# A decoder step's last stage: another order of its hand-written queues, other rooms for its weights, and per-layer inputs loaded ahead

## The chip, the cores and the metric

The kernel runs on one core of a Trainium2 chip, in one launch. The metric is device time in microseconds of that core. The version before was run three times: median 2211.37 us, 2208.99 to 2212.40. One more execution was recorded by the hardware profiler. It took 2207.24 us; all times "at" some microsecond below count from the start of its span of 2205.2 us.

The engines are TensorE (PE in the profile, its weight loads PEld), VectorE (DVE), ScalarE (ACT), GpSimd (POOL) and SyncE (SP), which here only issues DMAs. Each works through its own list in order.

## The reference, cut to what matters

The reference is one layer of a decoder: attention in two groups, a gated MLP with a short convolution, and a gate by per-layer inputs, for 1024 prompt tokens and 64 sample tokens. The change lies in the last two steps, the MLP's product with `w_down` and the per-layer gate:

```python
y = (jax.nn.silu(conv) * c) @ lw['ffn_w_down']
...
h = h + y
h = h + (p @ lw['ple_w_proj']) * jax.nn.sigmoid(rmsnorm(h, lw['g_ple']) @ lw['ple_w_gate'])
```

`h` is 1024 tokens by 1024 columns, `p` 1024 by 256, `ple_w_gate` 1024 by 1024, `ple_w_proj` 256 by 1024, all float32.

## The kernel before, in words

**Products.** A float32 product is done as three products of rounded parts: an operand is split into a high part (a cast, mostly on ScalarE) and a low part (operand minus high part, on VectorE), and `mm3` (L160 to L163) multiplies high by high, high by low and low by high. Both `w_down` and `ple_w_gate` are multiplied by a scheme of seven products of quarter matrices in place of eight, with sums and differences of quarters as operands.

**The down pass** (loop over `steps`, from L2388) does its seven products one after the other, in the order `SEVEN`, each in eleven steps `k`. Step `k` multiplies for four tiles of 128 tokens, `t` = 0 to 3. The last product is `p == 4`. Its steps 9 and 10 are done together, tile by tile. After each tile's last step `folded` adds the sum from PSUM to `h` (L2330), on VectorE. Between the steps of this last product the kernel already prepares the next stage: `square` and `root` make the row scales of the norm (ScalarE, then GpSimd), `turn_first` transposes a first quarter of `h` (`xg`, `r11`), and `ple_in(c)` brings in one of two chunks of the per-layer inputs: three DMAs into tiles named `pin` (two of four token tiles, one of the 64 sample rows), transposes on TensorE (L2364), splits into `ph`, `pl` and `pts`. Chunk 0 is called at `k == 5`, chunk 1 after tile 0 of the last step. Each `ple_in` issues its own loads, into the three rooms of the `stage` ring. After the loop four `square`, `root` and four stores `dh<-h` (L2436) follow.

**The last stage** multiplies by `ple_w_gate`. Its instructions are put in by name: `later(name, make)` notes a step, and the string `LAST` (L39) lists all names. Inside `manual_schedule` the steps of TensorE, ScalarE, VectorE and GpSimd keep the order of that string on their engine. SyncE isn't in that list; the order of its DMAs is the compiler's choice, as is where the instructions outside `LAST` (`ple_in`, `turn_first`) come in between. The names that matter:

| name | engine | what it does |
|---|---|---|
| `P1t` to `P7t` | TensorE | product 1 to 7 for tile t: 12 matmuls of 512 columns |
| `Yt`, `Tbt`, `Tat` | TensorE | turns of three quarters of `h`, four transposes each, all into the three banks `pd` |
| `Jnt`, `sA`, `sB`, `sJf` | TensorE | projection of `p` (6 matmuls); sample rows (8, 8 and 4 matmuls) |
| `ryt`, `rat`, `Ut` | ScalarE | copies from banks to `h`: of `Yt` (L2542), of `Tat`, of `P1t` |
| `it`, `et`, `gt`, `jt` | VectorE | sums and differences of turned quarters; `it`, `et` read the bank of `Tbt` |
| letter + `c` or `l` + number | ScalarE / VectorE | high and low part of an operand (`ac0`/`al0` of tile 0, `wc0`/`wl0` of a weight row block) |
| `JL`, `W`, `C`, `Z`, `V`, `N`, `X` | SyncE | loads of weights (`wp`, `wn`), 512 KB each |
| `csk`, `ck`, `zk`, `vk`, `nk` | ScalarE / VectorE | scale by the gain and subtract quarters of weights |
| `jc0_`, `jl0_` | ScalarE / VectorE | parts of `ple_w_proj`, 1024 columns |
| `Cq`, `Cs`, `Cm`, `Ca`, `Co` | VectorE, ScalarE, SyncE | sum, sigmoid, times projection, plus `h`, store |
| `sk0`, `sd0` | VectorE / ScalarE | empty the bank of `sJ0` |

**Rooms.** The weight loads go through four rooms in turn (`pair`, L2444): `gb` in the pool `hp`, `pc` in the pool `pl`, and two rooms of the down pass, `place_of(10)` and `r4`. The n-th load takes room n modulo 4, and waits until whoever used that room before is done with it. The pool `pl` is opened when the down pass's pool `wf` is closed, over the same memory: `sg`, `wj`, the rooms `q3k` and `q2k` of the split weights, and `pc` last. Banks of PSUM come from four small rings: `pd` (three banks), `pm` (two), `p2t` (two), `p2` (one). `turn_first` and `ple_in` take theirs from `p2t`.

Of the kernel before, what the change touches and what calls it, by code (L numbers as in the profile page):

```python
# [8 lines left out]
F32 = mybir.dt.float32  # L9
# [9 lines left out]
P = 128  # L19
D = 1024  # L20
T = 1024
NT = 8
NB = 8
TS = 8
R = NB * TS
# [13 lines left out]
LAST = (  # L39
# [13 lines left out]
VIAP = 20  # L53
GS0 = 1
NWB = 10
# [11 lines left out]
def step_kernel(ctx: ExitStack, tc: tile.TileContext, A):  # L67
    nc = tc.nc
    pe, act, dve, pool, sp = nc.tensor, nc.scalar, nc.vector, nc.gpsimd, nc.sync
# [151 lines left out]
    z = {}  # L221
# [1189 lines left out]
    def stage(shape, dt, name):  # L1411
        return z["sg"].tile(shape, dt, tag="stage", name=name, bufs=3)
# [67 lines left out]
    def square(t, f):  # L1480

        rows = P if t < NT else R
        junk = z["junk"].tile([P, 512], BF16, tag="junk", name="junk")
        act.activation(junk[:rows], hrows(t)[:, f * 512:f * 512 + 512], AF.Square, scale=1.0 / 32.0,
                       accum_out=z["ss"][:rows, 2 * t + f:2 * t + f + 1])
# [7 lines left out]
    def root(t):  # L1493

        rows = P if t < NT else R
        s0, s1 = (z["ss"][:rows, 2 * t + f:2 * t + f + 1] for f in range(2))
        pool.tensor_scalar(s0, s0, s1, EPS, ALU.add, ALU.add)
        return pool.tensor_tensor(z["rs"][:rows, t:t + 1], s0, mhalf[:rows, 0:1], ALU.pow).ins
# [156 lines left out]
    def p2t(shape, name):  # L1655
        return psT.tile(shape, F32, tag="t", name=name)
# [319 lines left out]
    def later(name, make):  # L1976

        steps[name] = make
# [210 lines left out]
    def part(i, j, t):  # L2189
        return h[:, 4 * i + t, j * 512:j * 512 + 512]  # L2190

    def kept(i, j, t):
        return dh2[(4 * i + t) * P:(4 * i + t + 1) * P, j * 512:j * 512 + 512]
# [4 lines left out]
    def turn_part(i, j, t, bank, here=False):  # L2198
        pt = bank([P, 4, P], "pt")
        for k in range(4):  # L2200
            m = pe.transpose(pt[:, k], part(i, j, t)[:, k * P:(k + 1) * P], ident)
            if here and k == 0:
                tc.keep_in_program_order(m)
        return pt
# [13 lines left out]

    def turn_first(t):

        pt = turn_part(0, 0, t, p2t, True)
        xg["11", t] = x = xroom(room_tag(0, t))
        split(x[:, 0], x[:, 1], pt)
        if t % 2 == 0:
            r11[t // 2] = z["xs"].tile([P, 2, 512], F32, tag=place_of(4 + t // 2), name="r11", bufs=1)
        act.copy(v4(r11[t // 2][:, t % 2]), pt)
# [36 lines left out]
    def place_of(k):  # L2263
        return f"st{(k + 3) % NK}"
# [50 lines left out]
    def folded(p, t):  # L2315

        ps = acc[p][t]
        h11, h12, h21, h22 = (h[:, i, j:j + 512] for i in (t, t + 4) for j in (0, 512))
        if p == 1:
            act.copy(h11, ps)  # L2320
        elif p == 5:
            act.copy(h22, ps)
            act.copy(h12, ps)
        elif p == 6:
            dve.tensor_tensor(h21, h11, ps, ALU.add)
        elif p == 7:
            dve.tensor_tensor(h21, h21, ps, ALU.subtract)
        else:
            hx = {3: h12, 2: h11, 4: h21}[p]
            dve.tensor_tensor(hx, hx, ps, ALU.add)  # L2330
# [9 lines left out]
    def ple_gain():  # L2340
# [5 lines left out]
        z["gk"] = z["fb"].tile([P, 8], F32, name="gkT", tag="gkT")  # L2346
        act.copy(z["gk"], pt[:, 0:8])

    def ple_in(c):

        th, tl = (z["fq"].tile([P, T], F32R, tag="p" + s, name="p" + s, bufs=2) for s in "hl")
        cs = slice(c * P, (c + 1) * P)
        for t0 in (0, 4, 8):
            pin = stage([P, 4, P], F32, "pin")
            if t0 < NT:
                n, rows = 4, P
                sp.dma_start(pin, A["p_prompt"][0, 0, t0 * P:(t0 + 4) * P, cs].rearrange("(i p) c -> p i c", p=P))
            else:
                n, rows = 1, R
                sp.dma_start(pin[:R, 0], A["p_sample"][0].rearrange("b t c -> (b t) c")[:, cs])  # L2360
            pt = p2t([P, 512], "pt_pl")
            w = (n - 1) * P + rows
            for i in range(n):
                pe.transpose(pt[:, i * P:i * P + rows], pin[:rows, i], ident[:rows, :rows])  # L2364
            if t0 < NT:
                split(th[:, t0 * P:t0 * P + w], tl[:, t0 * P:t0 * P + w], pt[:, :w])
            else:
                ts = z["fq"].tile([P, P], F32R, tag="pts", name="pts", bufs=2)
                split(ts[:, :R], ts[:, R:], pt[:, :R])
        return th, tl, ts  # L2370
# [17 lines left out]
    for i, (p, k) in enumerate(steps):  # L2388
        if i + 4 < len(steps):
            load(*steps[i + 4])  # L2390
        if i + 2 < len(steps):
            operands(*steps[i + 2])
        if k == 0:
            acc[p] = banks(i // NK)
        q = SEVEN[i // NK - 1] if i >= NK else 0
        if p == 4 and k == NK - 2:
            continue
        for t in range(4):
            for k_ in ((k - 1, k) if p == 4 and k == NK - 1 else (k,)):
                summed(p, k_, t)  # L2400
            if k == NK - 1:
                folded(p, t)
            if p == 4 and k == NK - 1 and t == 0:
                pT.append(ple_in(1))
        if q and k in (1, 3, 5, 7):
            folded_on(q, k // 2)
        for p0, k0, i_, j_ in ((6, 2, 1, 1), (3, 3, 0, 0), (2, 1, 0, 1), (2, 2, 1, 0)):
            if p == p0 and k >= k0 and (k - k0) % 2 == 0 and k - k0 < 8:
                residue(i_, j_, (k - k0) // 2)
        if p == 1 and k == 1:  # L2410
            with tc.issue_after(opd[-1][0]):
                for half in range(2):
                    fold_sample(acc_s[half], half)
        elif p == 1 and k == 4:
            row_scale(NT)
            ple_gain()
        elif p == 1 and k == 7:
            turned_sample()
        elif p == 2 and k == 8:
            first_gate()  # L2420
        elif p == 4:
            if k in (1, 3, 5, 7):
                row_scale(k // 2)
                square(k // 2 + 4, 1)
            if k in (2, 4, 6, 7):
                turn_first((k - 1) // 2)
            if k in (6, 8):
                for t in range(4):
                    i_ = (8 - k) // 2
                    sp.dma_start(kept(i_, 1, t), part(i_, 1, t))  # L2430
            if k == 5:
                pT.append(ple_in(0))
    for t in range(4):
        square(t + 4, 0)
        root(t + 4)
        sp.dma_start(kept(1, 0, t), part(1, 0, t))  # L2436

    rw.close()
    opened("pl")
# [3 lines left out]

    def pair():  # L2444

        pool_, tag = ((z["hp"], "gb"), (z["pl"], "pc"), (z["xs"], place_of(10)), (z["xs"], "r4"))[pairs[0] % 4]
        pairs[0] += 1
        return pool_.tile([P, 2, 512], F32, tag=tag, name="wp", bufs=1)

# [56 lines left out]
        later(f"{name}l{k}", lo)  # L2506

    def tile_part(t):

        def s2():  # L2510
            return r11[t // 2][:, t % 2]
# [323 lines left out]
```

## Time and profile before

| | before |
|---|---|
| median of three runs | 2211.37 us |
| runs | 2208.99 to 2212.40 us |
| profiled execution | 2207.24 us |
| its span | 2205.2 us |
| TensorE busy, share of span | 2117.2 us, 96% |
| VectorE | 1701.4 us, 77% |
| ScalarE | 1384.4 us, 63% |
| granted TensorE clock, mean | 0.987 |

In a timeline a row gives the start, the duration, the engine and line, the operation, what it writes and reads, and how often in a row; in brackets the idle time of the engine before it and what ended that. Matmuls are pipelined: a row lasts longer than the distance to the next start, and the distance is what counts. A table by stage gives, for each stretch, the busy time and the number of instructions (in parentheses) of each engine, the granted TensorE clock (1.00 is full), the share of the DMA engines in use and their rate. A row of waits gives who waited for whom, the sum in us, how many times, and the longest. In the row of 40 slices a digit is the busy share of a slice of 55 us in tenths.

### The profile page before, as it was taken

To read this page: it belongs to the slowest core of one execution; us is meant where nothing else is said; L and a number is where in the kernel's file an instruction comes from. 1 tells how busy PE (TensorE), PEld (TensorE's weight loads), DVE (VectorE), ACT (ScalarE), POOL (GpSimd) and SP (SyncE) were. 2 spreads that over 40 slices of the span, in tenths; PEclk is the share of its full clock that TensorE was granted. 3 is DMA by queue.
4 is the path that set the end of the run, shared out by engine and by line. 5 is a ranking of instruction groups with operands and counts; after the bars stand their busy time and mean duration, and the time that the engine had idled before them with its cause. 6 is when DMAs were issued, how large, how long until landed. Compare 5 with 4: busy or idle time off the path is not lost. (4 is left out here: it accounts for less than half of the span.)

```text
span 2205.2 us, 37408 instructions
## 1 busy us (share of the span) xinstructions
PE 2117.2 (96%) x12928; PEld 1897.3 (86%) x12928; DVE 1701.4 (77%) x2611; ACT 1384.4 (63%) x3735; POOL 1207.0 (55%) x1311
## 2 busy tenths in 40 slices
PE   7999999999999999999999999999999999999799
PEld 6888978878888888887898878999999998888677
DVE  4775676467788888887788878888888886996686
ACT  5676766777778888887777776433333333534651
POOL 5675668576777777778455556565656651001100
PEclk9999999999999999999999999999999999999899
DMA  5343235412342222211421223323222226878432
GB/s 186 107 144 108 77 120 157 142 54 68 106 121 58 63 75 62 61 56 47 161 88 58 84 82 98 110 86 102 91 92 95 92 82 235 248 219 251 141 126 84
DMA packets 205952, 244.56 MB, mean 111 GB/s; under 512 B 42934, under 2 KB 137635, under 8 KB 205763
## 3 DMA queue, kind: packets, MB, share of 16 engines
q1 hardware_dynamic: 189507, 189.98, 27.3%
q0 software_dynamic: 15024, 47.72, 7.5%
q10 hardware_dynamic: 1232, 4.46, 0.5%
q8 instruction: 104, 1.70, 0.3%
q14 instruction: 85, 0.70, 0.1%
HBM read 196.39 MB, written 45.67 MB: 110 GB/s over the span
## 5 line engine op out<-in xcount | busy, mean ns | idle before, releaser
L582 ACT ACTIVATE csq<-ks 128x256 f32<-128x256 f32 x1040 | 392.7, 400 | 91.9 <-PE ks L163 82.0
L587 DVE TENSOR_REDUCE css<-csq 128x16 f32<-128x1024 f32 (+1 forms) x264 | 315.6, 1196 | 60.4 <-ACT csq L582 59.3
L137 ACT CAST wh<-st 128x512 fp32r<-128x512 f32 x164 | 100.9, 619 | 170.4 <-PE ps_gu L162 158.6
L161 PE MATMUL ks<-mv0h,cTh 128*128 128x320 f32 (+1 forms) x520 | 171.7, 332 | 7.8 <-ACT sn L584 3.8
L161 PE MATMUL ks<-mv1h,cTh 128*128 128x320 f32 (+1 forms) x520 | 170.4, 329 | 7.7 <-ACT sn L584 3.5
L627 POOL TENSOR_TENSOR chl<-craw,chl 128x1024 fp32r<-128x1024 f32 x64 | 141.5, 2212 | 56.5 <-ACT chl L625 54.7
L162 PE MATMUL ks<-mv1l,cTh 128*128 128x320 f32 (+1 forms) x520 | 153.8, 298 | 0.0
L162 PE MATMUL ks<-mv0l,cTh 128*128 128x320 f32 (+1 forms) x520 | 152.7, 295 | 0.0
L163 PE MATMUL ks<-mv0h,cTl 128*128 128x320 f32 (+1 forms) x520 | 148.3, 298 | 0.9 <-DVE cTl L138 0.8
L163 PE MATMUL ks<-mv1h,cTl 128*128 128x320 f32 (+1 forms) x520 | 148.5, 299 | 0.1
L655 POOL TENSOR_TENSOR phl<-sn,phl 128x512 fp32r<-128x512 f32 (+1 forms) x63 | 84.1, 1335 | 84.5 <-ACT phl L652 84.1
L138 DVE TENSOR_TENSOR wl<-st,wh 128x512 fp32r<-128x512 f32 x124 | 108.6, 879 | 26.4 <-ACT wh L137 26.3
L162 PE MATMUL ps_dn<-o 128*128 128x512 f32 x308 | 120.2, 390 | 0.1
L163 PE MATMUL ps_dn<-o 128*128 128x512 f32 x308 | 119.9, 389 | 0.0
L138 DVE TENSOR_TENSOR cTl<-ctp,cTh 128x512 fp32r<-128x512 f32 (+1 forms) x136 | 90.0, 661 | 38.5 <-ACT cTh L137 37.5
L138 POOL TENSOR_TENSOR wl<-st,wh 128x512 fp32r<-128x512 f32 x40 | 62.6, 1564 | 103.8 <-ACT wh L137 99.1
L161 PEld LDWEIGHTS ks<-mv0h,cTh 128*128 128x128 f32 x520 | 98.6, 190 | 21.8 <-ACT sn L584 8.0
L161 PEld LDWEIGHTS ks<-mv1h,cTh 128*128 128x128 f32 x520 | 99.5, 191 | 20.0 <-ACT sn L584 7.9
L584 ACT COPY sn<-ks 128x64 f32<-128x64 f32 x520 | 116.7, 224 | 0.0
L161 PE MATMUL ps_dn<-o 128*128 128x512 f32 x308 | 114.7, 391 | 0.0
L1332 POOL TENSOR_TENSOR pl<-p,ph 128x512 fp32r<-128x512 f32 (+1 forms) x96 | 97.6, 1021 | 30.0 <-DVE ph L1331 20.7
L163 PE MATMUL ps_gu<-xrh,wl 128*128 128x320 f32 x352 | 108.8, 309 | 0.0
(738 smaller groups left out, 7722.3 us busy)
## 6 DMA issues: line engine op xcount, KB each, us to landing
raw<-ds SPq DMA_DIRECT2D x77, 256.0 KB
raw<-ffn_w_down SPq DMA_DIRECT2D x66, 256.0 KB
stage<-w_in SPq DMA_DIRECT2D x48, 256.0 KB
wr<-ffn_w_down SPq DMA_DIRECT2D x44, 256.0 KB
st<-ffn_w_gate SPq DMA_DIRECT2D x42, 256.0 KB
st<-ffn_w_up SPq DMA_DIRECT2D x42, 256.0 KB
ds<-cv SPq DMA_DIRECT2D x19, 512.0 KB
oraw<-doT SPq DMA_DIRECT2D x16, 256.0 KB
```

The source lines that it names most:

```text
L137: cast = act.copy(hi, src)
L138: res = (lo_eng or dve).tensor_tensor(lo, src, hi.bitcast(F32), ALU.subtract)
L161: pe.matmul(ps, ah, bh, start=first, stop=False)
L162: pe.matmul(ps, ah, bl, start=False, stop=False)
L163: return pe.matmul(ps, al, bh, start=False, stop=last)
L582: act.activation(sq[:, f * 256:f * 256 + 256], ks[:, 0:256], AF.Square)
L584: act.copy(o.sn[:, g0 + i, :], ks[:, 256:320])
L587: dve.tensor_reduce(o.ss[:, g0 + i + 1 - n:g0 + i + 1, :].rearrange("p i h -> p (i h)"), sq2[:, :n].rearrange("p i (h n) -> p (i h) n", n= ...
L627: pool.tensor_tensor(ch[:, c0:c1, 128:256], src, ch[:, c0:c1, 0:128].bitcast(F32), ALU.subtract)
L655: (dve if drain == 2 else pool).tensor_tensor(phl[:, :nt, 64:128], sb, phl[:, :nt, 0:64].bitcast(F32), ALU.subtract)
L1332: pool.tensor_tensor(pl[:, c0:], p[:, c0:], ph[:, c0:].bitcast(F32), ALU.subtract)
```

## The change

Four things change. The string `LAST` gets another order, and takes in the last folds of the down pass, the squares, the roots and the stores of four tiles (`ft`, `sqt`, `rtt`, `stt`), which stood outside. The lists of TensorE in the two strings are the same. The four rooms of the weight loads are taken in another rotation. The loads of both chunks of per-layer inputs are issued at step 4 of the last product, chunk 1 into `gb` and `gtile`, and the chunks are turned at steps 6 and 8. `turn_first` and the sample part of `ple_in` use `pm` banks in place of `p2t`.

On ScalarE the string now begins `sq0 sq1 cs0 wc3 wc2 wc1 wc0 sq2 cc0 sq3 jc0_ ry0 U0 ra0 ac0 ic0 ec0 ry1`, before it was `jc0_ wc0 wc1 wc2 wc3 cs0 cc0 cs1 cc1 cs2 ry0 ac0 ra0`. On VectorE it begins `f0 f1 c0 f2 wl3 wl2 wl1 wl0 cl0 f3 jl0_ i0 e0 al0 g0 il0 i1 e1`, before `jl0_ wl0 wl1 wl2 wl3 c0 cl0 c1 cl1 i0 c2 e0`.

The diff, with the string cut to its beginning and the place of `V1` and `JL1`:

```diff
 LAST = (
-    "JL0 jc0_ W0 jl0_ wc0 W1 wc1 wl0 wl1 wc2 C0 wc3 wl2 wl3 C1 cs0 c0 cc0 cl0 cs1 C2 c1 P10 cc1 cl1 Y0 Tb0 cs2 Ta0 "
-    "C3 i0 ry0 P11 c2 ac0 ra0 e0 ic0 g0 cc2 al0 Y1 U0 Tb1 cl2 Z0 ry1 Ta1 i1 P12 cs3 e1 U1 g1 ic1 ac1 j0 ra1 Y2 al1 "
...
-    "Cq3 gl3 Cs13 Co11 Cm12 sJ0 zc1 Ca12 zc0 P70 zl1 sd0 Co12 zl0 z2 V1 so zs2 Cm13 zc2 yc0 Ca13 P71 sc0 zl2 Co13 "
-    "yl0 v2 Z3 sk0 vc2 sl0 yc1 P72 vl2 ss0 yl1 hy0 sm0 z3 P73 N1 yc2 sa0 zs3 yl2 zc3 v3 zl3 cv vc3 hy2 nc0 vl3 yc3 "
-    "n3 JL1 P60 nc1 n2 nc3 nl1 nc2 nl3 cvc hy1 P61 nl0 nl2 jc0 X0 yl3 jl0 P62 u0 jc1 u1 jl1 ha0 P63 X1 u2 jc2 jl2 "
+    "JL0 W0 f0 sq0 st0 rt0 W1 f1 C0 sq1 rt1 st1 cs0 c0 wc3 f2 wc2 wl3 st2 wc1 wl2 wc0 wl1 sq2 wl0 cc0 rt2 cl0 P10 f3 "
+    "sq3 st3 rt3 jc0_ Y0 Tb0 ry0 jl0_ Ta0 U0 P11 ra0 i0 C1 ac0 e0 ic0 al0 ec0 g0 Y1 il0 Tb1 ry1 Ta1 i1 U1 P12 ac1 e1 "
+    "C2 cs1 al1 ra1 g1 ec1 j1 ic1 Y2 j0 Tb2 ry2 Ta2 il1 U2 P13 c1 ac2 C3 cs2 el1 cc1 al2 ra2 c2 Y3 i2 cc2 el0 ry3 "
+    "ic2 cl2 Z0 cs3 il2 e2 c3 Tb3 ec2 Ta3 U3 e3 sA cc3 i3 ac3 cl3 ic3 al3 ec3 J10 il3 pA ra3 z0 J11 cl1 zs0 g3 V0 "
...
+    "N0 v1 Ca11 vc1 P23 Cq2 gc2 vl1 Cs12 Co11 gl2 Cm12 Z2 n0 sB gc3 n1 gl3 sJ0 Cq3 zc0 zc1 so P70 sd0 zl0 sc0 zl1 V1 "
+    "Cs13 z2 Cm13 zs2 Ca13 P71 yc0 sl0 zc2 Co13 yl0 ss0 zl2 Z3 v2 yc1 sk0 vc2 yl1 P72 vl2 sm0 hy0 sa0 z3 N1 P73 yc2 "
+    "Ca12 zs3 yl2 zc3 v3 zl3 vc3 hy2 cv yc3 vl3 nc1 yl3 P60 JL1 nc0 nl1 cvc n3 n2 nc3 nl0 P61 nc2 hy3 nl3 jc0 nl2 "
...
-        pt = turn_part(0, 0, t, p2t, True)
+        pt = turn_part(0, 0, t, pm, True)
...
+    pins = {}
+
+    def pin_load(c):
+
+        cs = slice(c * P, (c + 1) * P)
+        if c == 0:
+            x = [stage([P, 4, P], F32, "pin") for _ in range(3)]
+        else:
+            x2 = z["hp"].tile([P, 2, 4, P], F32, tag="gb", name="pin", bufs=1)
+            x = [x2[:, 0], x2[:, 1], const.tile([P, 1, P], F32, tag="gtile", name="pin")]
+        for i in range(2):
+            sp.dma_start(x[i], A["p_prompt"][0, 0, 4 * i * P:(4 * i + 4) * P, cs].rearrange("(i p) c -> p i c", p=P))
+        sp.dma_start(x[2][:R, 0], A["p_sample"][0].rearrange("b t c -> (b t) c")[:, cs])
+        pins[c] = x
...
-        for t0 in (0, 4, 8):
-            pin = stage([P, 4, P], F32, "pin")
...
+        for j, pin in enumerate(pins[c]):
+            n, rows = (4, P) if j < 2 else (1, R)
+            t0 = 4 * j
+            pt = (p2t if j < 2 else pm)([P, 512], "pt_pl")
...
-            if k == NK - 1:
+            if k == NK - 1 and p != 4:
                 folded(p, t)
-            if p == 4 and k == NK - 1 and t == 0:
-                pT.append(ple_in(1))
...
-            if k == 5:
-                pT.append(ple_in(0))
-    for t in range(4):
-        square(t + 4, 0)
-        root(t + 4)
-        sp.dma_start(kept(1, 0, t), part(1, 0, t))
+            if k == 4:
+                for c in range(2):
+                    pin_load(c)
+            if k in (6, 8):
+                pT.append(ple_in(k // 8))
...
-        pool_, tag = ((z["hp"], "gb"), (z["pl"], "pc"), (z["xs"], place_of(10)), (z["xs"], "r4"))[pairs[0] % 4]
+        pool_, tag = ((z["pl"], "pc"), (z["xs"], place_of(10)), (z["xs"], "r4"), (z["hp"], "gb"))[pairs[0] % 4]
...
+        later(f"f{t}", lambda: folded(4, t))
+        later(f"sq{t}", lambda: square(t + 4, 0))
+        later(f"rt{t}", lambda: root(t + 4))
+        later(f"st{t}", lambda: sp.dma_start(kept(1, 0, t), part(1, 0, t)))
```

More of the change, by code (lines that the diff above doesn't have):

```diff
@@ L2347, in ple_gain @@
         act.copy(z["gk"], pt[:, 0:8])
+    pins = {}
[10 more added lines that the diff above has]
+        pins[c] = x
     def ple_in(c):
         th, tl = (z["fq"].tile([P, T], F32R, tag="p" + s, name="p" + s, bufs=2) for s in "hl")
-        cs = slice(c * P, (c + 1) * P)
-        for t0 in (0, 4, 8):
-            pin = stage([P, 4, P], F32, "pin")
[L2355 to L2361, printed above, removed]
+        for j, pin in enumerate(pins[c]):
+            n, rows = (4, P) if j < 2 else (1, R)
+            t0 = 4 * j
+            pt = (p2t if j < 2 else pm)([P, 512], "pt_pl")
             w = (n - 1) * P + rows
@@ L2364, in ple_in @@
                 pe.transpose(pt[:, i * P:i * P + rows], pin[:rows, i], ident[:rows, :rows])
-            if t0 < NT:
+            if j < 2:
                 split(th[:, t0 * P:t0 * P + w], tl[:, t0 * P:t0 * P + w], pt[:, :w])
```

15 rows, old and new, of the table LAST are left out of this document.

## The prediction

> **What bounds the kernel now.** I read the page first, for where TensorE is not full, then a table by stage of that place, then the waits of TensorE there, then the timelines of the engines that it waited for.
>
> ```profile
> span 2205.2 us, 37408 instructions
> PE   7999999999999999999999999999999999999799
> ```
>
> TensorE is full in every slice but the first and the 38th (2040 to 2095 us), where the down pass ends and the last stage begins. The table by stage cuts that region:
>
> ```profile
> core 0: us, PE busy (x) PEld busy (x) DVE busy (x) ACT busy (x) POOL busy (x), PEclk, DMA share, GB/s
> 2069.40:2080.40 11.00, 0.04 (x1) 0.00 (x0) 7.89 (x12) 7.30 (x13) 0.00 (x0) 0.58 0.62 187
> 2080.40:2085.00 4.60, 4.38 (x16) 3.46 (x17) 4.53 (x8) 4.60 (x10) 0.00 (x0) 0.52 0.47 161
> 2085.00:2121.80 36.80, 35.39 (x162) 27.66 (x160) 33.37 (x54) 22.61 (x38) 0.00 (x0) 1.00 0.35 110
> 2121.80:2126.10 4.30, 0.00 (x1) 0.03 (x1) 1.49 (x3) 0.71 (x2) 0.00 (x0) 0.97 0.49 187
> 2126.10:2129.20 3.10, 3.10 (x7) 2.44 (x8) 3.10 (x6) 1.16 (x2) 0.00 (x0) 0.50 0.60 184
> 2133.50:2200.10 66.60, 66.34 (x299) 53.90 (x297) 44.68 (x68) 19.04 (x32) 0.00 (x0) 1.00 0.28 94
> 2070.60:2133.90 63.30, 47.56 (x206) 37.38 (x207) 53.09 (x83) 38.35 (x67) 0.00 (x0) 0.87 0.43 139
> ```
>
> Two holes, of 11.0 and 4.3 us, each followed by a stretch at half clock (0.52, 0.50). Between them TensorE and VectorE are both above 90% busy. From 2133.5 on TensorE has no hole, so what is won must be won before that. Who ended the holes:
>
> ```profile
> PE pt L2201 <- ACT h L2542: 11.2, 2, 11.0
> PE ps_pg L161 <- ACT wg L2494: 4.3, 1, 4.3
> PE ps_pj L161 <- DVE sg L2603: 0.9, 1, 0.9
> ```
>
> The first hole ends with `ry0` (L2542): the turns `Y1` need the bank that `Y0` filled, and `ry0` empties it. ScalarE's timeline shows why that is late:
>
> ```profile
> 2069.47 0.21 ACT L137 CAST pts<-pt_pl 128x64 fp32r<-128x64 f32 x1 [2.73 <-PE pt_pl L2364]
> 2069.58 1.05 ACT L2674 CAST wj<-wp 128x1024 fp32r<-128x1024 f32 x1
> 2070.53 2.56 ACT L2496 ACTIVATE wg<-wp,gkT 128x512 fp32r<-128x512 f32 x4
> ...
> 2079.18 0.72 ACT L2635 ACTIVATE wp<-wp,gkT 128x512 f32<-128x512 f32 x1 [1.27 <-DMA wp<-ple_w_gate]
> 2079.81 0.57 ACT L2542 COPY h<-pt 128x512 f32<-128x512 f32 x1
> ```
>
> ScalarE is in order. It stood until 2069.47 for the second chunk of per-layer inputs, which TensorE turned late, then did `jc0_`, four `wc`, `cs0`, `cc0`, `cs1`, `cc1`, and held at `cs2` for a load. `ry0` was queued behind all of it. TensorE around it:
>
> ```profile
> 2061.30 0.40 PE L161 MATMUL ps_pg<-wg,xg 128*128 128x512 f32 x1
> 2064.10 0.92 PE L2201 MATMUL pt<-ident,h 128*128 128x128 f32 x7
> 2066.20 0.48 PE L161 MATMUL ps_pg<-wg,xg 128*128 128x512 f32 x1
> 2069.16 0.27 PE L2364 MATMUL pt_pl<-ident,pin 64*128 64x64 f32 x1
> 2080.43 2.09 PE L2201 MATMUL pt<-ident,h 128*128 128x128 f32 x8 [10.99 <-ACT h L2542]
> 2133.55 0.48 PE L161 MATMUL ps_pg<-wg,xg 128*128 128x512 f32 x1
> ```
>
> `P10` starts at 2061.30 and takes 2.80 (12 matmuls, 0.233 each). Between 2064.10 and 2066.20 lie 20 transposes, 0.105 each, 8 of them of the second chunk. `P60` starts at 2133.55, 72.25 us after `P10`. The work between: 12 products (33.6), 48 transposes (5.0), 9 pin transposes (1.1), 4 projections of six (5.6), 20 sample matmuls (4.7), `cv` (0.4): 50.4. So 21.8 us are holes and lost clock, and no reordering can win more.
>
> The second hole:
>
> ```profile
> 2116.90 7.69 DMA wp<-ple_w_gate
> 2124.61 0.75 DVE L2638 SCALAR_TENSOR_TENSOR wp<-wp,gkT 128x512 f32<-128x512 f32 x1 [4.01 <-DMA wp<-ple_w_gate]
> 2126.10 0.76 PE L161 MATMUL ps_pg<-wg,xg 128*128 128x512 f32 x1 [4.31 <-ACT wg L2494]
> ```
>
> The load `V1` left at 2116.90 and landed 7.69 later. VectorE stood at `v2` for it, and `sk0`, next in its queue, empties the bank that `P72` wants. The waits name a cast of ScalarE, but the bank is what the code makes `P72` wait for.
>
> **The change, part by part.** TensorE's own list is untouched, so only what feeds it moves.
>
> *Second chunk ahead.* In the code before, its `pin` tiles took rooms of the first chunk's; now they have their own (`gb`, `gtile`), are issued at step 4 of the down pass's last product, and are turned at step 8 instead of among `P10` and `P11`. The 1.1 us of transposes move into the down pass, which then ends 1.1 later, and leave the stage: zero on TensorE. What it wins is ScalarE's and VectorE's wait until 2069.5. The splits (two of 512 columns, one of 64) land where ScalarE and VectorE also make the last operands. They are covered if those operands stay ahead. Uncovered they cost at most their own time on VectorE, this row and a short third:
>
> ```profile
> 2066.12 1.35 DVE L138 TENSOR_TENSOR pl<-pt_pl,ph 128x512 fp32r<-128x512 f32 x2 [3.77 <-ACT ph L137]
> ```
>
>
> *Rooms rotate by one.* `JL0` goes to `pc`, `W0` and `W1` to rooms of the down pass, `C0` to `gb` after the pins.
>
> ```profile
> 2047.87 1.28 SPq L2631 DMA_DIRECT2D wp<-ple_w_gate  x3
> 2049.25 3.78 SPq L2357 DMA_DIRECT2D pin<-p_prompt  x2
> 2062.75 0.43 SPq L2631 DMA_DIRECT2D wp<-ple_w_gate  x1
> 2071.91 0.33 SPq L2631 DMA_DIRECT2D wp<-ple_w_gate  x1
> ```
>
> and one of SP's own waits:
>
> ```profile
> SPq L2631 <- DVE wj L2678: 8.7, 1, 8.7
> ```
>
> The three loads of 2047.87 (`C0` in two, `W1`) took the down pass's rooms; `W0` and `W1` now go about then. The load into `pc` was the one at 2062.75, when the down pass was over. `JL0`, next in that room, I put there too. `C1` waited 8.7 us for `jl0_` to free its room, and still must.
>
> *New order of the queues.* The folds of the down pass:
>
> ```profile
> 2056.50 0.69 DVE L2330 TENSOR_TENSOR h<-h,ps_dn 128x512 f32<-128x512 f32 x1 [2.39 <-PE ps_dn L163]
> 2057.28 0.63 ACT L1484 ACTIVATE junk<-h 128x512 bf16<-128x512 f32 x1 [3.92 <-DVE h L2330]
> 2057.82 0.19 ACT L1484 ACTIVATION_READ_ACCUMULATOR junk<-h 128x1 f32 x1
> 2057.86 0.69 DVE L2330 TENSOR_TENSOR h<-h,ps_dn 128x512 f32<-128x512 f32 x1 [0.67 <-PE ps_dn L163]
> 2058.57 1.03 PE L2201 MATMUL pt<-ident,h 128*128 128x128 f32 x8
> ```
>
> A square is 0.75 with the read of its sum (2057.28 to 2058.01). The eight transposes of 2058.57 (0.8) and the pins (1.1) now come ahead, so `f1` goes from 2057.86 to 2059.8. ScalarE from its end, 2060.5: `sq1` 0.75, `cs0` 0.72, four `wc` 2.56, `sq2` 0.75, `cc0` 0.6 (a copy like `ry0`): 2065.9. `sq3` needs `f3`, which VectorE does after `cl0` (2 x 0.62): 2067.1. `sq3` 0.75, `jc0_` 1.05, `ry0` 0.57: `ry0` ends at 2069.5. TensorE: down pass 2062.4, `P10` 2.8, 12 transposes 1.3, `P11` 2.8: `Y1` is due at 2069.3. The first hole shrinks to 0.2 us.
>
> What is late next is VectorE. `c0` adds a wait, for `cs0` and so for `C0`'s load; `f2`, the `wl`, `f3` and by them `st2`, `st3` are queued behind it. `jl0_` runs from 2068.9 to 2070.1. `Tb1` needs `e0`, second behind it: 2071.3, a hole of 1.4. `Ta1` needs `al0`, the third: 2071.9, 0.2 more. TensorE is then at 2072.4, and with `P12`, `P13` and 16 transposes at 2079.7, before `Tb3`. That needs `e2`, the 21st behind `jl0_`: 2070.1 + 21 x 0.618 = 2083.1, and 0.4 for ScalarE's `ic2`: 2083.5, a hole of 3.8.
>
> A hole of 4.3 was paid with 3.1 us at 0.50, so 1.55; one of 0.9 with nothing. The 3.8 is nearer to the first: I take 1.4, ends 0 and 1.55. [...]
>
> *The sum.* VectorE is the bound: from `jl0_` to `vl3`, which `P60` needs, it has 77 instructions; the row of 2070.60 has 83 from `jl0_` on, because six (`wl0` to `wl3`, `c0`, `cl0`) stood behind `jl0_` and are now ahead of it. At 33.37/54 = 0.618 each, and 0.6 more for the double-width `jl0_`, that is 48.2. It starts when `jc0_` ends, 2068.9. Added: 1.4 for the half clock, by which `Cq0` waits longer for `P20`, and 1.5 for `V1` (ends 0 and 4.0, the wait it had). I take less than 4.0 because the list now frees `V1`'s room before `JL1`'s, 512 KB fewer ahead of it. So `vl3` ends at 2068.9 + 48.2 + 2.9 = 2120.0, against 2134 before, where the 83rd of that row ends: **14.0 us** earlier. From there the lists of all engines are nearly the old ones, and VectorE is only 67% busy there (44.68 of 66.60), so I carry the gain to the end unchanged. The moved stores and roots cost nothing: what needs them, the first sigmoid and the reloads of `h`, comes over 20 us later.
>
> The profiled execution took 2207.24, span 2205.2 and 2.0 around it; the median of the runs is 2211.37, 4.1 above. I take the gain from the median: **2197.4**.
>
> Ends: `jl0_` could start 1.2 earlier (if `f3` doesn't hold `sq3`) or 4.6 later (if `JL0` leaves only behind the fourth store, at 2067.4, and takes 5 of `V1`'s 7.7 us). With `V1` at 0 or 4.0, the half clock at 0 or 1.55 and, at the bad end, the splits uncovered (1.6), the gain is 5.2 to 18.1, so 2193.3 to 2206.2.
>
> **Rivals.** *The pace stays.* VectorE stood 10.2 of 63.3 us in the row of 2070.60, part of it for loads. If the four rooms still feed it no faster, `P60` comes 62.9 us after `jl0_` as before (2133.55 - 2070.66), from 2068.9 at 2131.8: 1.8 won, 2209.6, no change. For it: `C1`, `C2`, `C3` and `V0` still wait for rooms. Against: before, much of that wait was ScalarE's, ahead of `ry0`.
>
> *The queue's head is blocked: slower.* `JL0` is first in SP's list, and its room lies where the one load of 2062.75 went. If SP waits there for the down pass, `W0`, `W1`, `C0` and `JL0`, 2 MB, start at 2062.8; at the 187 GB/s of the first hole's row they are in at 2074.0. From `cs0` to `jl0_` were 7.7 us: `jl0_` at 2081.7. The rooms then turn over at the old pace, so `P60` at 2144.6, 11.0 late: 2222.4. It decides at the old pace from `jl0_` at 2070.7 on; at my pace only from 2082.9. Against: SP's order before let the three loads pass ahead of the one into `pc`.
>
> *No half clock.* If a hole of 3.8 is too short to be paid for, as 0.9 was, the gain is 15.4: 2196.0. [...]
>
> *It doesn't do what it says.* The pins are still turned behind `P10`, because TensorE's list is mixed with theirs by the compiler; then `jc0_` again follows 2069.5 and the gain is some 1.5 smaller, inside the range.
>
> **How the numbers follow.** The forecast has 0.82, with the last two cases in it (0.3 without the half clock, 0.07 with pins behind `P10`). The pace that stays has 0.09. The blocked head has 0.09, of which 0.02 within 0.2%, since a queue blocked for less costs less. About 0.2% (4.4 us) is what a measurement of this kernel can tell from no change. Faster: 0.82. Same: 0.09 + 0.02 = 0.11. Slower: 0.07. The range is the likeliest case's, 2193.3 to 2206.2, rounded out to 2193 and 2207; what it leaves out is those two rivals and little more.
>
> **What would show it.** Right: the hole before `ry0` gone, `jl0_` near 2069, `pt_pl` all before `P10`, VectorE over 95% busy from 2069 to 2118, a hole of about 4 us before `Tb3`, `P60` near 2120. Wrong: `JL0` or `C0` issued after 2064, ScalarE idle at `cs0` or `jc0_`, a load-bound VectorE near `c1` or `v2`, or holes in the down pass before 2061.

## The result, and the profile after

The median of the changed kernel is 2198.79 us (5 runs, 2197.16 to 2201.02) against 2211.37 (5 runs by then, with the median of the first three); the ratio is 0.9945, 95% interval 0.9930 to 0.9959, so 9.1 to 15.5 us faster. Timed once more beside the experiments it was 0.9953 (0.9940 to 0.9965). The forecast was 2197.4, 14.0 faster.

The profiled execution took 2200.6, with a span of 2198.6. The second line has TensorE's tenths over the span; the 38th slice, which held the hole before `Y1`, reads 9 now. The hole before `P72` lies in the 39th, which read 9 before and after.

```profile
span 2198.6 us, 37402 instructions
PE   7999999999999999999999999999999999999998
```

One correction comes first. These two rows, of before and of after, are the first turn of `h` in the down pass (`turn_first`, start and duration in us):

```profile
2036.27 0.38 PE L2201 MATMUL pt<-ident,h 128*128 128x128 f32 x2
```

```profile
2039.86 0.38 PE L2202 MATMUL pt<-ident,h 128*128 128x128 f32 x2
```

The change gives TensorE nothing to do ahead of it, yet it is 3.6 later, and near 285 us in the span the two executions already lie some 4 us apart: start times of two executions can't be subtracted. I compare distances from `P10`. Table by stage of after:

```profile
core 0: us, PE busy (x) PEld busy (x) DVE busy (x) ACT busy (x) POOL busy (x), PEclk, DMA share, GB/s
2066.09:2077.00 10.91, 8.60 (x48) 6.79 (x47) 8.65 (x13) 9.18 (x18) 3.52 (x5) 1.00 0.84 255
2077.00:2099.00 22.00, 20.86 (x101) 16.21 (x99) 21.01 (x35) 15.58 (x29) 0.00 (x0) 1.00 0.28 96
2116.40:2119.20 2.80, 0.00 (x0) 0.00 (x0) 1.46 (x3) 1.24 (x2) 0.00 (x0) 0.96 0.88 336
2119.20:2122.50 3.30, 3.27 (x8) 2.62 (x9) 3.27 (x6) 0.00 (x0) 0.00 (x0) 0.52 0.77 234
2126.70:2192.90 66.20, 66.20 (x299) 53.87 (x296) 44.22 (x67) 19.40 (x32) 0.00 (x0) 1.00 0.29 95
2073.50:2127.20 53.70, 46.20 (x206) 36.07 (x207) 48.23 (x78) 34.40 (x61) 0.12 (x1) 0.97 0.47 154
```

The waits of TensorE in the last stage (total, times, longest):

```profile
PE ps_pg L162 <- ACT wg L2501: 2.9, 1, 2.9
PE ps_pj L162 <- DVE sg L2615: 1.5, 1, 1.5
PE pt L2202 <- ACT h L2554: 1.4, 2, 0.9
PE pt L2202 <- DVE sg L2558: 1.4, 1, 1.4
PE pt L2202 <- ACT h L2570: 0.5, 1, 0.5
```

The hole of 11.0 before `Y1` is one of 0.9, and the half clock behind it (a granted clock near 0.5) is gone. New are 1.4 before `Tb1` and two of 0.5; the hole before `J13` grew from 0.9 to 1.5. The hole before `P72` is still there, 2.85 for 4.31, with its half clock (0.52). From `P60` on TensorE is busy throughout, as before. The timeline has the instructions of the argument:

```profile
2066.09 0.39 PE L162 MATMUL ps_pg<-wg,xg 128*128 128x512 f32 x1
2071.85 0.63 ACT L1485 ACTIVATE junk<-h 128x512 bf16<-128x512 f32 x1 [1.73 <-DVE h L2331]
2073.42 0.57 ACT L2554 COPY h<-pt 128x512 f32<-128x512 f32 x1
2073.54 1.23 DVE L2690 TENSOR_TENSOR wj<-wp,wj 128x1024 fp32r<-128x1024 f32 x1 [1.79 <-ACT wj L2686]
2079.67 0.72 ACT L2647 ACTIVATE wp<-wp,gkT 128x512 f32<-128x512 f32 x1 [1.59 <-DMA wp<-ple_w_gate]
2097.61 1.28 ACT L2603 ACT_TABLE_LOAD   x1 [2.16 <-DVE sg L2598]
2099.66 0.69 DVE L2615 TENSOR_TENSOR sg<-sg,ps_pj 128x512 f32<-128x512 f32 x1 [0.88 <-ACT sg L2603]
2117.74 0.75 DVE L2650 SCALAR_TENSOR_TENSOR wp<-wp,gkT 128x512 f32<-128x512 f32 x1 [1.95 <-DMA wp<-ple_w_gate]
2119.23 0.76 PE L162 MATMUL ps_pg<-wg,xg 128*128 128x512 f32 x1 [2.85 <-ACT wg L2501]
2124.40 0.69 DVE L2490 TENSOR_TENSOR xg<-h,xg 128x512 fp32r<-128x512 f32 x1 [1.59 <-ACT xg L2486]
2126.70 0.48 PE L162 MATMUL ps_pg<-wg,xg 128*128 128x512 f32 x1
```

From the top: `P10`; `sq3`, which stood 1.73 for `f3`; `ry0`; `jl0_`; `cs1`, which stood 1.59 for `C1`'s load; the sigmoid's table load ahead of `Cs10`; `Cm10`; `v2`, which stood 1.95 for `V1`; `P72`; `yl2`; `P60`. From `P10` to `P60` it is 60.61 us, for 72.25 before: 11.6 less. The first turn lies 26.23 ahead of `P10`, for 25.03: the second chunk's turns, now in the down pass, cost 1.2 there. So the profile shows 10.4 won; a second profile of the same kernel (e9 below) shows 11.6. The timed 12.6 holds both in its interval.

### The profile page after: what moved, and what is told of

Read it like the earlier page. It is cut to its first block, busy times and chain, and to the rows that moved or that the text cites. A ratio compares the mean times of both kernels' runs of the same rounds, so it can differ in the third digit from the quotient of the medians.

```text
span 2198.6 us, 37402 instructions
## 1 busy us (share of the span) xinstructions
PE 2118.3 (96%) x12928; PEld 1897.4 (86%) x12928; DVE 1704.7 (78%) x2611; ACT 1381.8 (63%) x3735; POOL 1207.0 (55%) x1311
## 4 chain that ended last, share of the span: by engine, by line
PE 77%; DVE 8%; ACT 5%; DMA 4%; POOL 3%; issue 2%; SPq 0%; DVEq 0%; POOLq 0%; ACTq 0%
PE ps_gu L163 7%; PE ps_gu L164 7%; PE ps_gu L162 7%; PE ks L162 5%; PE ks L164 4%; PE ks L163 4%; PE ps_dn L163 3%; PE ps_dn L164 3%; PE ps_dn L162 3%; PE cpv L671 2%; PE ctp L545 2%; PE ps_lt L301 2%; PE ps_pj L162 1%; PE ps_pj L163 1%; PE ps_pj L164 1%
```

## The experiments

All runs in one table. Times in the middle are us from `P10`'s start in each kernel's single profile; "turns" is from the first turn to `P10`; the last columns are the median and the ratio to the kernel before with its interval.

| kernel | turns | jl0_ | cs1 | P20 | P72 | P60 | us | ratio |
|---|---|---|---|---|---|---|---|---|
| before | 25.03 | 9.36 | | 36.38 | 64.80 | 72.25 | 2211.4 | 1 |
| changed | 26.23 | 7.45 | 13.58 | 25.69 | 53.14 | 60.61 | 2198.8 | 0.9945 (0.9930-0.9959) |
| e9, the same again | 26.23 | 7.51 | 13.84 | 25.96 | 53.46 | 59.49 | 2199.3 | 0.9953 (0.9940-0.9965) |
| e1 old order | 26.24 | 6.22 | | 33.27 | 61.58 | 69.16 | 2209.7 | 0.9995 (0.9983-1.0007) |
| e2 late turn | 24.98 | 9.37 | 14.39 | 28.53 | 55.93 | 61.96 | 2203.1 | 0.9960 (0.9944-0.9976) |
| e3 more VectorE | 26.24 | 7.34 | 13.58 | 29.30 | 56.23 | 63.62 | 2203.8 | 0.9964 (0.9951-0.9977) |
| e4 C0 free | 26.44 | 7.11 | 13.58 | 25.70 | 52.72 | 60.12 | 2200.8 | 0.9954 (0.9936-0.9971) |
| e5 ry0 first | 26.24 | 6.25 | | 33.31 | 61.93 | 69.51 | 2211.0 | 0.9995 (0.9983-1.0006) |
| e6 sk0 first | 26.24 | 7.52 | 13.26 | 25.38 | 50.14 | 56.17 | 2196.8 | 0.9931 (0.9915-0.9948) |
| e7 V1's room | 26.24 | 7.38 | 14.04 | 26.16 | 51.58 | 57.59 | 2196.7 | 0.9921 (0.9904-0.9937) |
| e8 table early | 26.24 | 7.33 | 13.15 | 25.28 | 51.75 | 59.30 | 2200.1 | 0.9939 (0.9922-0.9956) |
| e10 f3 early | 26.23 | 5.59 | 13.56 | 25.68 | 52.86 | 58.90 | 2201.6 | 0.9962 (0.9950-0.9975) |
| e11 together | 26.28 | 5.28 | 13.38 | 26.04 | 49.81 | 55.83 | 2194.4 | 0.9934 (0.9918-0.9950) |
| e12 C1's room | 26.95 | 5.27 | 10.23 | 22.86 | 46.65 | 52.67 | 2192.5 | 0.9922 (0.9908-0.9936) |

The distances tell apart what the times can't: the intervals reach 2.5 to 3.9 us to either side, so smaller effects are read from the profile, one execution of each kernel. How far two executions of one kernel differ the two profiles of the changed kernel show: 0.3 at `P20`, and 1.1 the other way at `P60`. The medians of e2, e3, e4, e5, e8 and e10 came 1.0 to 3.7 us above the times that were expected of them, also where the distances came as expected; most of those times had been reckoned from one median, 2198.79.

My theory: the gain comes from the order of ScalarE's and VectorE's queues ahead of `Y1`, and VectorE then sets the pace. Rivals: the second chunk's early turn is the gain; loads set the pace.

**e1: everything but the order.**

```
-LAST = "JL0 W0 f0 sq0 st0 rt0 W1 f1 C0 sq1 ..."
+LAST = "JL0 jc0_ W0 jl0_ wc0 W1 wc1 wl0 ..."   (the order before; folds, squares, roots, stores as before)
```

> Pins ahead and rooms rotated, but the stage's old order of the queues, folds, squares and stores as before. Theory (the gain is ScalarE's queue in front of ry0): ry0 again stands behind jc0_, four wc, cs0, cc0, cs1, cc1 and cs2, that is 7 to 11 us behind jc0_'s start near P10 + 7; a hole of 7 to 11 us before Y1, P60 at P10 + 68 to 73, and the time 2207 to 2213. Rival (the second chunk's early turn is the gain): no hole before Y1 over 2 us, P60 near P10 + 61, and 2197 to 2203.

Its waits of TensorE:

```profile
PE pt L2202 <- ACT h L2554: 8.7, 2, 8.5
PE ps_pg L162 <- ACT wg L2505: 4.2, 1, 4.2
```

The hole before `Y1` is back with 8.5, though the second chunk was turned long before. From first turn to `P72` it wins 2.0 us (89.8 to 87.8) where the changed kernel wins 10.5 (79.4). The first rival falls: pins and rooms without the order win 2.0 us by the profile, and by the times 1.1, with no change inside the interval.

**e2: the order, with the second chunk turned late.**

```
+later("pi0", ...); later("pi2", ...)      # second chunk's turns and splits, loaded into r2
-"... rt3 jc0_ Y0 Tb0 ry0 jl0_ Ta0 U0 P11 ra0 ..."
+"... rt3 pi0 Y0 Tb0 Ta0 P11 pi2 jc0_ ry0 jl0_ U0 ra0 ..."
```

> The new order and rooms, but the second chunk (loaded into room r2) is turned between P10 and P11 and, its last part, behind P11, as in the kernel before. Theory: ScalarE has pts behind P11 and so jc0_ near P10 + 8 and ry0 1 to 2 us later than in the changed kernel; the down pass is 1.1 shorter; P60 at P10 + 61 to 63.5, time 2198 to 2201.5. Rival (the early turn is the gain): the hole before ry0 is back with over 6 us and the time is 2207 or more.

`P60` came at 61.96, inside the theory's bounds; the median, 2203.1, is above them, with 2199.0 to 2206.1 as its ratio's interval. `P72` is the fairer mark (below, on the clock): from first turn to `P72` it is 80.9, for 79.4 and 79.7 of the changed kernel. The early turn is worth 1.2 to 1.5 us at most, the order and the rooms the rest. At most, because in e2 the holes of 1.73 and 1.00 ahead of `P12` were followed by half clock, 0.50 from 2081.70 to 2085.00 in its profile, and the 0.90 and 1.41 of the changed kernel were not; how much of that lasts to `P72` isn't shown.

**e5: only `ry0` moved, in e1.**

```
-"JL0 jc0_ W0 jl0_ wc0 ... C2 c1 P10 cc1 cl1 Y0 Tb0 cs2 Ta0 C3 i0 ry0 P11"
+"JL0 P10 Y0 jc0_ ry0 W0 jl0_ wc0 ... C2 c1 cc1 cl1 Tb0 cs2 Ta0 C3 i0 P11"
```

> The kernel of e1 (old order, with pins and rooms) with one thing moved: P10 and Y0 in front of jc0_ and ry0 right behind it, so that ry0 no longer stands behind the casts and scalings. Theory (not ry0 alone: the whole queues have to be turned round, since VectorE's i0 and e0, which free the bank of Tb1, still stand behind c1 and cl1, which wait for loads): the hole moves from Y1 to Tb1, 6 to 9 us there, P60 at P10 + 66 to 69.5, time 2207 to 2210. Rival (ry0 was the one instruction that held the stage, as the list of waits names it): no hole over 3 us before Tb1, P60 at P10 + 60 to 63, time 2200 to 2204.

```profile
PE pt L2202 <- DVE sg L2558: 8.7, 1, 8.7
PE ps_pg L162 <- ACT wg L2505: 4.5, 1, 4.5
```

The hole is as long as before, 8.7 us, one step further: `Tb1` waits for `e0` (L2558), which stands behind `c1` and `cl1` on VectorE. The wait that the list names is only the first in line.

**e3: six VectorE instructions twice.**

```
-"... al0 ... il0 ... al1 ... il1 ... el1 ... cl2 ..."
+"... al0 al0 ... il0 il0 ... al1 al1 ... il1 il1 ... el1 el1 ... cl2 cl2 ..."
```

> The changed kernel with six VectorE instructions done twice (al0, il0, al1, il1, el1, cl2; the second writes the same values), 6 x 0.62 = 3.7 us of work between jl0_ and the Tb3 turns. Theory (VectorE paces the stretch from jl0_ to vl3): P60 comes 2.5 to 3.7 later, at P10 + 63.1 to 64.3, time 2201.3 to 2202.5. Rival (loads and the rooms pace it, VectorE has 5.5 us idle there): at most 1 us later, 2198.8 to 2199.8.

`P20` is 3.6 later, `P72` 3.1, `P60` 3.0, of 3.7 added. The loads are the same, and the added work of VectorE moves `P20` by almost its whole length: VectorE sets the pace there, and the rival, loads with 1 us at most, falls. (Ahead of `c1` a load does hold it, see e10.)

**e4: `C0` not behind the second chunk.**

```
-x2 = z["hp"].tile(..., tag="gb", name="pin", bufs=1)
+x2 = z["xs"].tile(..., tag="r2", name="pin", bufs=1)
```

> The changed kernel with the second chunk in room r2 instead of gb, so that the load C0 need not wait for its turns. Theory: C0 lands before cs0 wants it, ScalarE's idle 1.2 before cs0 goes, jl0_ starts at P10 + 6.5 to 7.0 instead of 7.45, and P60 comes 0.5 to 1.0 sooner: 2197.8 to 2198.4. Rival (JL0 itself, in pc, which opens with the end of the down pass, gates jc0_): C0 early, but jl0_ and P60 within 0.2 of the changed kernel, 2198.8.

`jl0_` is 0.34 earlier, less than I expected, and `P20` unmoved (25.70). `P60`'s 0.5 came later, from a hole before `P72` of 2.42 for 2.85. Up to `P20` the rival is right: nothing is won.

**e6 and e7: the hole before `P72`.** e6 moves one name, e7 one room.

```
-"... Z3 v2 yc1 sk0 vc2 ..."                                     (e6)
+"... Z3 sk0 v2 yc1 vc2 ..."
+V1 in place_of(5), loaded behind gl3; N1 in gb, V1's old room   (e7)
```

> The changed kernel with sk0, which frees the bank for P72, moved in front of v2 on VectorE. Theory: the hole of 2.85 before P72 and the 1.5 us of half clock behind it go, but P60 then waits for vl3 on VectorE, whose end (1.6 us ahead of P60's need) moves by 0.6 at most: P60 1.0 to 2.2 us sooner, at P10 + 58.4 to 59.6, time 2196.6 to 2197.8. Rival (TensorE alone pays for that hole): 4.0 to 4.4 sooner, P10 + 56.2 to 56.6, 2194.6.

> The changed kernel with V1 in the room that gl3 frees (N1 takes V1's), and loaded right behind gl3 instead of behind zl0. Theory (room, not bandwidth): V1 is issued 2 to 4 us earlier, v2's wait of 1.95 goes, the hole before P72 is under 1.2 us and full clock follows, and P60 comes 2.0 to 3.6 us sooner, at P10 + 57.0 to 58.6, time 2195.2 to 2196.8. Rival (the loads share the bandwidth: an earlier V1 lands only as early as before, since Z2 and N0 are on their way): v2 still waits over 1.5 us, gain under 0.7.

In e6 `P60` came 4.4 sooner than in the changed kernel and 3.3 sooner than in e9: the rival's figure, not mine, though the median, 2196.8, lies nearer to mine. Counted from `P20`, ahead of which the edit does nothing, it is 4.1 and 2.7. VectorE did not hold `P60`. Its stand of 1.59 at `yl2` in the changed kernel went too: `yl2` waits for a cast of ScalarE, and that cast waited 4.60 for the last matmuls of `P72`. So the late `P72` had made VectorE late, and not only VectorE the hole. In e9, with the hole but at full clock behind it, `yl2` followed at once, as in e6 (the first row is e9, the second e6):

```profile
2122.68 0.69 DVE L2490 TENSOR_TENSOR xg<-h,xg 128x512 fp32r<-128x512 f32 x1
```

```profile
2121.11 0.68 DVE L2490 TENSOR_TENSOR xg<-h,xg 128x512 fp32r<-128x512 f32 x1
```

e7 went as expected at its end: no stand at `v2`, a hole of 0.8, `P60` at 57.59. But `V1` left only 1.0 us sooner after `P10`, not 2 to 4. It left ahead of `N1` instead of behind it, so the room and the order of the loads aren't told apart.

**e8: the sigmoid's table early.**

```
+later("TS", lambda: act.preload_act_table_set("sigmoid_and_others"))    # behind pA
```

> The changed kernel with the sigmoid's table loaded early, behind pA, instead of in front of Cs10. Theory (the load of 1.28 us is exposed between Cq0 and Cs10, and VectorE's Cm10 and TensorE's J13 wait for it): the hole before J13 falls from 1.50 to 0.2 to 0.6, VectorE's stand before Cm10 of 0.88 goes, and all behind it, V1's load too, comes 0.6 to 1.3 us sooner: P60 at P10 + 59.3 to 60.0, time 2197.5 to 2198.2. Rival (something later takes it back: V1's landing or the bank for P72 stays where it is): J13's hole gone but P72 and P60 within 0.3 of the changed kernel.

The hole before `J13` fell from 1.5 to 0.5. `P72` came 1.4 to 1.7 sooner than in the two profiles of the changed kernel, but 0.4 to 0.7 of that lies ahead of `P20`, where the edit does nothing; from `P20` to `P72` it is 1.0, the length by which the hole shrank. `P60` came at the early end of what was expected.

**e9 to e11: `f3` early, and all together.**

```
-"... wc3 f2 wc2 wl3 ... cl0 P10 f3 sq3 ..."
+"... wc3 f2 f3 wc2 wl3 ... cl0 P10 sq3 ..."      (e10; e11 has it with e4, e6, e7, e8)
```

> The changed kernel once more, as the measure for the next two. Every theory: ratio to the kernel before 0.993 to 0.996, P60 at P10 + 60.3 to 60.9.

The ratio came as expected, `P60` 0.8 us sooner than that: no half clock followed the hole before `P72` this time.

> The changed kernel with f3 right behind f2 on VectorE, in front of the wl instructions and cl0, so that sq3 and behind it jc0_ and ry0 need not wait for it. Theory (f3 holds sq3, ScalarE's idle 1.73 there, and by it jc0_ and jl0_, and VectorE passes it on): jl0_ at P10 + 5.7 to 6.1 instead of 7.45, the hole of 0.9 before Y1 gone, P60 0.9 to 1.6 us sooner, at P10 + 59.0 to 59.7, 2197.2 to 2197.9. Rival (JL0, issued only as the down pass ends, gates jc0_, or C1's load gates VectorE behind it): jl0_ not before P10 + 6.9, or P60 within 0.3 of the changed kernel.

> All the edits that helped or were neutral together: f3 early, V1 in gl3's room, sk0 in front of v2, the sigmoid's table early, the second chunk in r2. Theory (they act on different waits, so they add up from e6's P10 + 56.2: f3 0.9 to 1.4, the table 0.5 to 1.0, C0 0.3): P60 at P10 + 53.5 to 54.8, time 2191.0 to 2193.5. Rival (VectorE's 48.2 us of work is the floor: jl0_ at P10 + 5.9, 48.2 and one us of waits put the end of vl3 at P10 + 55.1 and P60, which needs it 2.3 later than its start, cannot lie under P10 + 52.8; but other waits, C1's load above all, keep it over P10 + 55.5): time 2194 to 2196.

In e10 `jl0_` started 1.9 earlier, a little more than expected, the hole before `Y1` went, and `P20` started at the same 25.68. Why, its timeline and chain of waits say (`C1`'s load from issue with its duration, then `cs1`, then the stage's transfers):

```profile
2082.10 6.14 DMA wp<-ple_w_gate
```

```profile
2088.32 0.72 ACT L2647 ACTIVATE wp<-wp,gkT 128x512 f32<-128x512 f32 x1 [3.43 <-DMA wp<-ple_w_gate]
```

```profile
2078.50:2088.25 9.75, 8.60 (x49) 6.85 (x47) 8.47 (x13) 6.39 (x13) 3.63 (x4) 1.00 0.73 229
```

And of the changed kernel:

```profile
2075.18 4.41 DMA wp<-ple_w_gate
```

`C1` left at `P10` + 7.34 instead of + 9.09, because `jl0_` freed its room sooner, but took 6.14 instead of 4.41, and landed at 13.5 in both; other loads were under way meanwhile, 229 GB/s in that stretch. `cs1` starts at 13.2 to 14.0 in nine of the ten profiles that the table has it for before e12 (14.39 in e2, where ScalarE was late). Here the rival was right: a load is the gate between `jl0_` and `c1`. e11 ended at 55.83 and 2194.4, past my bounds and within the rival's, for this reason: `ra1`, behind `cs1` on ScalarE, came late for `Ta2`, a hole of 1.94 with half clock behind it.

By time e10 is no faster than e9 (0.9962 and 0.9953, intervals that overlap); by the profile 0.6, half of it already there at `P20` and half a shorter hole before `P72`.

**e12: `C1` and `C2` exchange rooms, in e11.**

```
-"... ra0 i0 C1 ac0 ... ac1 e1 C2 cs1 ..."
+"... ra0 i0 C2 ac0 ... ac1 e1 C1 cs1 ..."
```

> The kernel of e11 with the loads C1 and C2 exchanged in the list of loads, so that C1 takes W0's room, free some 3 us after P10's start, and C2 takes JL0's, free after jl0_. Theory (from jl0_ on, C1's load sets the pace: cs1 started at P10 + 13.2 to 14.0 in every kernel of this study with the second chunk turned early, whether jl0_ began at 5.3 or 7.5; it is issued behind C2 and C3 and shares the transfer with them): cs1 starts at P10 + 10 to 11.5, VectorE's stand of 2.7 in front of j goes, and P60 comes 1.8 to 2.7 us sooner than in e11, at P10 + 53.1 to 54.0, time 2191.5 to 2192.8. Rival (the bandwidth itself is the floor there: whichever load comes last lands at P10 + 13.4, and C2 now holds the queues instead): cs2 waits, and P60 is not under P10 + 55.3.

`cs1` starts at 10.23, and VectorE has no hole left. The two stretches are from `jl0_` to 8.6 us behind `P60`, and from `P20` to `P60` (columns as in the table by stage):

```profile
2074.30 0.72 ACT L2653 ACTIVATE wp<-wp,gkT 128x512 f32<-128x512 f32 x1 [0.42 <-DMA wp<-ple_w_gate]
```

```profile
2069.34:2125.30 55.96, 54.24 (x249) 42.65 (x248) 54.83 (x89) 38.73 (x69) 1.86 (x3) 1.00 0.54 171
2086.93:2116.74 29.81, 29.02 (x125) 22.53 (x124) 29.65 (x49) 17.99 (x29) 0.00 (x0) 1.00 0.60 197
```

VectorE does 89 instructions in 55.96 us, 54.83 of them busy. But TensorE is busy for 54.24 of the same stretch. The prediction counted 50.4 us of work for TensorE from `P10` to `P60`, and the way is 52.67 now, so only 2.3 us of holes are left there. VectorE has no wait left to take away, and TensorE hardly any; which of the two is the bound these runs don't show. `P60` comes 3.2 sooner than in e11, all of it ahead of `P20`: the hole of 1.94 and its half clock are gone. Against e9 it is 6.8 (0.7 of it is lost ahead of `P10`). The rival, that `cs2` then waits for the exchanged load, fell: ScalarE had no idle time before `cs2`.

At 0.9922 this version is 14.1 to 20.3 us faster than the kernel before, and faster than e9, whose interval lies apart from its own. From e6, e7 and e11 (0.9931, 0.9921, 0.9934) the times don't tell it apart; that it is the best of them rests on one profile each.

Not tried, and so open: the new order with the rooms unrotated, and the last sums in their old place with the rest of the new order. What the rotation alone is worth I can't say.

## Why the prediction was right, and where it was not

**The first hole.** Right in place and cause: `ry0` behind ScalarE's queue. 0.2 was forecast, 0.9 came; e1 and e5 show that order, not pins, took the hole away, and that VectorE's order had to change with ScalarE's, as the part on the new order had it.

**The pins.** 1.1 on the down pass was forecast, 1.2 came. They were turned ahead of `P10`; that rival did not happen.

**`jl0_`.** Forecast at `P10` + 6.5, came at + 7.45: `f3` held `sq3` for 1.73. The prediction had this wait as its other end, 1.2; e10 finds 1.9. But the sum let the end of `vl3` follow the start of `jl0_` one for one, and that was wrong: e10 gets 1.9 at `jl0_` and nothing at `P20`, because `C1` lands at + 13.5. The prediction named `C1`'s wait and gave it no price. By luck the two hid each other: in the changed kernel VectorE lost only 0.7 for `C1`.

**`Tb1` and `Tb3`.** 1.4 before `Tb1`: right to the digit, waiting for `e0` as said. The 3.8 before `Tb3`, and 1.4 of half clock, did not come. I had let the three banks be taken in strict turn; `Tb3` took one that ScalarE had emptied and waited 0.5 for `ra2` (L2570). It ran at 2085.33, and `e2`, for which the forecast had it wait, only at 2087.64.

**VectorE's 48.2.** Busy 48.23 from `jl0_` to `vl3` (the row of 2073.50): right, but 90% of that stretch, not over 95. The waits in it were put at 2.9 and were 5.5: 0.7 for `C1`, 0.9 for the table, 1.95 at `v2`, 1.59 at `yl2`, 0.3 in small ones. The table load was in the profile of before and left out of the sum; e8 prices it at 1.0.

**`V1`, the term most wrongly sized.** 1.5 was forecast on VectorE. The load took 6.22 for 7.69, and VectorE stood 1.95. But the cost ran over TensorE: 2.85 of hole and, in this execution, 1.5 of half clock, which held `yl2` in turn. e6 prices `P72`'s wait at 2.7 to 4.1. The prediction had seen in the profile of before that `sk0`, not `v2`, was what `P72` wanted, and then costed only VectorE's side.

**The sum.** The end of `vl3` was due at `P10` + 57.6 and came at 61.1: `jl0_` 0.95 late, the waits 2.6 longer. `P60` starts 0.5 ahead of it, at 60.61; in e9, without the half clock, at 59.49. So 14.0 forecast, 10.4 and 11.6 in the profiles, 12.6 timed: the right sign and size, with `V1` and `C1` underpriced and `Tb3` overpriced. That the size came out so near is partly luck: the 1.4 of half clock that was put down for `Tb3` came behind `P72` instead, where the sum had none.

**The rivals.** The pace that stays: no, `P60` lies 53.2 us behind `jl0_`, not 62.9. The blocked head: SP did stand, at `C0`, for the second chunk's turns,

```profile
SPq L2643 <- PE pt_pl L2374: 9.1, 1, 9.1
```

but with `W0` and `W1` already out and `JL0`'s room not yet open nobody needed what stood behind it; e4 takes the wait away and wins almost nothing.

## What to carry to other kernels

A wait names the first instruction in an ordered queue that is late, not the only one: move it alone and the next takes its place (8.7 us again in e5), so read the queue behind it to its end on every engine before pricing a reordering. When an instruction that frees a bank stands behind one that waits for a load, put it ahead; it costs one word and was worth 2.7 to 4.1 us here (e6). Where a room opens late, ask what else has been sent by then: `C1` left 1.75 us earlier and landed no sooner (e10), and only an exchange with a load that was not urgent moved it (e12: `cs1` at 10.23 instead of 13.38).

## What the runs showed of the hardware

After a short hole TensorE sometimes had half clock for some 3 us, and sometimes not. Table by stage, the hole before `P72` and the 3.3 us behind it, in e9, which is the changed kernel again, and in e3:

```profile
2116.05:2118.95 2.90, 0.00 (x1) 0.03 (x1) 1.49 (x3) 1.24 (x2) 0.00 (x0) 1.00 0.90 340
2118.95:2122.25 3.30, 3.30 (x14) 2.70 (x15) 3.27 (x6) 0.23 (x1) 0.00 (x0) 1.00 0.74 236
```

```profile
2118.63:2120.96 2.33, 0.00 (x1) 0.03 (x1) 1.49 (x3) 1.24 (x2) 0.00 (x0) 0.91 0.78 297
2120.96:2124.26 3.30, 3.30 (x8) 2.63 (x9) 3.27 (x6) 0.00 (x0) 0.00 (x0) 0.54 0.76 232
```

2.90 us idle and full clock behind it (14 matmuls in 3.3 us); 2.33 idle and 0.54 (8 matmuls). The changed kernel itself had 2.85 and 0.52 the first time. Of seven profiles with a hole of 2.3 to 2.9 there (changed, e2, e3, e4, e8, e9, e10) four paid, some 1.4 us each (from `P72` to `P73` it is 4.2 to 4.3 in them), and three did not (e2, e9, e10: 2.88). The length doesn't decide it: 2.33, 2.42, 2.84 and 2.85 paid, 2.58, 2.80 and 2.90 did not. In e8 the first four matmuls behind the hole still ran at full clock, and the half clock came 1 us behind it. In e11 half clock followed a hole of 1.94 before `Ta2` (a matmul of this kind takes 0.39 at full clock). There 12 transposes lie around the hole, with 3.6 us from the last matmul of 512 columns to the next, so this row doesn't show that a hole of 1.94 alone is enough:

```profile
2078.53 1.10 PE L2202 MATMUL pt<-ident,h 128*128 128x128 f32 x4 [1.94 <-ACT h L2570]
...
2079.85 0.63 PE L163 MATMUL ps_pg<-wg,xg 128*128 128x512 f32 x1
```

For a hole of 3.8 the prediction put down 1.4. The hole that it priced came as 0.5, before `Tb3`, and of the shorter ones here, 2.3 to 2.9, four in seven paid. Why a given hole pays stays open.

The table load of 1.28 us was paid where it stood in ScalarE's queue. In the changed kernel it began at 2097.61, after 2.16 of idle time that ended with `Cq0`, whose result the sigmoid needs and the load does not: e8 had it run 5.6 us ahead of the sigmoid, and the hole before `J13` was 1.0 shorter.
